# Matrix sums of a hybrid block's MLP moved from GpSimd to VectorE, and its second query/key group moved ahead

## The chip, the cores and the metric

The kernel runs on one core of a Trainium2 chip. The engines are TensorE (PE, matrix products; PEld is its weight load), VectorE (DVE), ScalarE (ACT), GpSimd (POOL) and SyncE (SP, which issues most loads). The metric is device time in microseconds (us), lower is better.

## What is computed

One decoder block on 512 tokens of width 1024, in float32: an RMS norm, one wide input projection, two causal token mixers side by side, a gated sum, an output projection with residual, and a squared-ReLU MLP with residual.

```python
p = rms_norm(x, norm_mix_g) @ w_in
q_a, k_a, v_a, o_a, i_a, f_a, q_b, k_b, v_b, g_a, g_b = split(p)
qk_a = silu(causal_conv([q_a, k_a], conv_w))          # 4 taps
h_a = mlstm_chunkwise(*heads(qk_a), v_a, i_pre, f_pre)  # 8 heads, 64-wide keys
y_a = sigmoid(o_a) * head_rms_norm(h_a)
y_b = stick_breaking(norm(q_b), norm(k_b), v_b)       # 8 heads, 128 wide
y = sigmoid(g_a) * y_a + sigmoid(g_b) * y_b
x = x + y @ w_out
h2 = rms_norm(x, norm_mlp_g)
x = x + square(relu(h2 @ w_up)) @ w_down              # 1024 -> 4096 -> 1024
```

## The kernel before

Every matrix product is done in split precision. Each float32 operand is held as a rounded part (hi) and a remainder (lo), and `mm3` (L110 to L113) issues three matmuls for one product: hi with hi, hi with lo, lo with hi. Weights come in pieces of 512 KB: `stage` (L95) loads a piece into a buffer "raw" of which there are two, ACT copies it rounded (`whi`, L106), and DVE subtracts to get the remainder (`wlo`, L107). The second matmul group on a piece can't start before both are there.

The first part of the program is the projections and the mixers. They are cut into steps that the list `ORDER` names: `qka0`, `qka1` project the queries and keys of mLSTM heads 0 to 3 and 4 to 7 (four banks of PSUM each, evicted by ACT into `xc`, L332, then a convolution on DVE into tiles `cy` with tag "sy"); `r0` to `r7` (`decay`, L369) load a row of gate sums over all partitions into one of three places with tag "f5", mask it on POOL and take the exponential on ACT; `m0` to `m7` are mLSTM heads (`za` scores, multiplied with `rb` on DVE, split into `ph` and `pl`, then `pn`, evicted by ACT into `yq`, L410); `n0` and `n4` norm four heads; `qkb0` to `qkb3` project queries and keys of two stick-breaking heads each (four PSUM banks, evicted by DVE into `nat`, L450, normed with a square root on ACT over `ssq`); `T0` to `T3` transpose them on PE (`pt_qT`, `pt_kT`); `s0` to `s7` are stick-breaking heads; `va1`, `vb0`, `vb1` project values; `oa`, `ga`, `gb` project gates. `ORDER` is the order in which the program is written. A scheduler then orders the instructions of each engine by a simulated timeline, with offsets of priority for evictions and weight pieces, so the order on an engine is near that of `ORDER` but not the same.

The MLP is cut into four quarters g = 0 to 3 of 1024 hidden columns. Each of its products, 512 x 1024 by 1024 x 1024, is done as seven products of half size (Winograd's form, `wino`, L649), on sums and differences of the quadrants: for the weights POOL issues loads that add into a buffer already there (L661), which are then split again (`parts`, L632: `whi_p..` on ACT, L635, `wlo_p..` on DVE, L636). For the operand, `rows_rest` (L553) makes four sums S1 to S4 of quadrants in place, in tiles `uq` (in the first call `hq`), and splits each. It is called twice for the normed input `h2` and twice in each quarter, ten times in all. Up and down products of neighbouring quarters alternate on PE. In the names `wlo_p2up21`, p2 is the product's number, up or dn the matrix, 2 the quarter and 1 the half of the piece; `xdn`, `ydn`, `zdn` and `pp_xup`, `pp_yup`, `pp_zup` are PSUM sums, `s` and `acc` what they are added to (`add`, L692). I call the stretch where quarter g's hidden rows are made and the next products wait for them boundary g.

Of the kernel before, what the change touches and what calls it, by code (L numbers as in the profile page):

```python
# [51 lines left out]
ORDER = ("qka0 r0 r1 qka1 r2 r3 qkb0 m0 r4 m1 m2 r5 m3 r6 n0 va1 T0 m4 m5 qkb1 vb0 r7 m6 oa0 s0 m7 T1 s1 ga0 "  # L52
         "n4 s2 s3 qkb2 T2 qkb3 vb1 T3 s4 s5 oa1 gb0 s6 s7 x0 ga1 gb1").split()
# [3 lines left out]
def block_kernel(ctx: ExitStack, tc: tile.TileContext, x, norm_mix_g, w_in, b_if, b_gate, conv_w, mlstm_norm_g,  # L57
# [35 lines left out]
    last, load_pool = {}, [(wp, "raw", 2)]  # L93

    def stage(k2, srcs, name, ahead=None, pool_raw=None):  # L95

        with tc.high_priority(offset=AHEAD if ahead is None else ahead):
            p, tag, bufs = load_pool[0] if pool_raw is None else (pool_raw, "raw", 2)
            raw = p.tile([P, 2, 512], F32, tag=tag, name=f"raw_{name}{k2}", bufs=bufs)
            for c, ap in srcs:  # L100
                n = ap.shape[-1]
                last["load"] = nc.sync.dma_start(out=raw[:, :, c:c + n],
                                                 in_=ap.rearrange("(kk p) n -> p kk n", p=P)).ins
            hi = wp.tile([P, 2, 512], F32R, tag="whi", name=f"whi_{name}{k2}")
# [221 lines left out]
    def qka(i):  # L326
# [6 lines left out]
        y = [t2("sy", 5, f"cy{i}{o}") for o in range(4)]  # L333
# [49 lines left out]
    def mlstm_head(h, qk, v, rb):  # L383
# [16 lines left out]
        s = t2("sy", 5, f"s{h}")  # L400
# [73 lines left out]
    def sb_head(h, q, k, v):  # L474
# [34 lines left out]
        yb = t2("sy", 5, f"yb{h}")  # L509
# [43 lines left out]
    def rows_rest(A, q, a21, a22, *sl):  # L553
# [4 lines left out]
        pool.tensor_tensor(p["S3"], p["A11"], a21, ALU.subtract)  # L558
        pool.tensor_tensor(p["S2"], p["S1"], p["A11"], ALU.subtract)
        pool.tensor_tensor(p["S4"], p["A12"], p["S2"], ALU.add)  # L560
# [58 lines left out]
    load_pool[0] = (rd, "rawd", 8)  # L619
# [231 lines left out]
```

## Time and profile before

| | before |
|---|---|
| median of 3 runs | 845.93 us (845.5 to 846.26) |
| profiled run, device time | 846.01 us |
| span of its trace | 844.3 us |
| PE busy | 815.5 us (97%) |
| DVE busy | 632.4 us (75%) |
| ACT busy | 442.0 us (52%) |
| POOL busy | 217.7 us (26%) |

The span is the time from the first to the last instruction in the trace of one execution; the device time holds 1.7 us more. Busy shares are means over stages. PE's ends are modelled, so the share says how much of the span it had work in hand, not that it ran at its peak.

### The profile page before, as it was taken

The numbers are of one execution on the slowest core, as the hardware profiler recorded it, in microseconds if no ns is written. First come the engines' busy times: TensorE is split into PE (matmuls) and PEld (weight loads), VectorE is DVE, ScalarE is ACT, GpSimd is POOL, SyncE is SP. The second block draws the span as 40 slices with busy tenths as digits, with TensorE's granted clock in tenths as the row PEclk, the third lists the DMA queues.
The fourth block names the chain that finished last, engine by engine and source line by source line (L and its number), as shares of the span: only waits on it lengthen the run. The fifth ranks groups of instructions, "written<-read, shape, count | busy, mean of one in ns | idle before, by whom it ended". The sixth has DMA issues, their size and how long they took to land.

```text
span 844.3 us, 11460 instructions
## 1 busy us (share of the span) xinstructions
PE 815.5 (97%) x4366; PEld 697.1 (83%) x4366; DVE 632.4 (75%) x785; ACT 442.0 (52%) x649; POOL 217.7 (26%) x244
## 2 busy tenths in 40 slices
PE   7999998999999999999999998999999999999987
PEld 5877777788888788888888888988997999899766
DVE  5577999796548687645764659898689778988994
ACT  6337567755436564443553456666456545555521
POOL 3014145141211110011120106174216421641530
PEclk9999999999999999999999999999999999999999
DMA  8155343474233242431349406878956996698365
GB/s 206 48 129 173 94 122 104 99 176 81 45 81 100 51 125 76 100 74 53 82 133 330 102 23 176 201 150 173 222 165 142 203 221 165 132 212 212 50 115 135
DMA packets 62760, 111.54 MB, mean 132 GB/s; under 512 B 5161, under 2 KB 17497, under 8 KB 62706
## 3 DMA queue, kind: packets, MB, share of 16 engines
q1 hardware_dynamic: 43122, 69.32, 29.3%
q0 software_dynamic: 19584, 41.50, 25.6%
q8 instruction: 34, 0.56, 0.3%
q14 instruction: 20, 0.16, 0.1%
HBM read 108.63 MB, written 2.17 MB: 131 GB/s over the span
## 4 chain that ended last, share of the span: by engine, by line
PE 68%; DVE 14%; DMA 7%; issue 5%; ACT 4%; POOL 1%; SPq 0%; POOLq 0%; ACTq 0%; DVEq 0%
PE pp_qkb L111 3%; PE pp_qkb L112 3%; PE pp_qkb L113 3%; DMA raw_qka<-in_w_in_dram 2%; PE ydn L111 2%; PE pp_yup L111 2%; PE ydn L112 2%; PE ydn L113 2%; PE pp_yup L112 2%; PE pp_yup L113 2%; PE pp_vb L111 2%; PE pp_ga L111 2%; PE pp_ga L113 2%; PE pp_gb L112 2%; PE pp_ga L112 2%
## 5 line engine op out<-in xcount | busy, mean ns | idle before, releaser
L487 POOL TENSOR_SCALAR_AFFINE_SELECT b<-b 128x128 f32<-128x128 f32 x32 | 20.9, 674 | 171.2 <-ACT b L484 171.2
L661 POOL DMA_DIRECT2D raw_Xup<-in_w_up_dram x24 | 29.1, 1230 | 110.6 <-DVE wlo_p1up L636 57.5
L661 POOL DMA_DIRECT2D raw_Xdn<-in_w_down_dram x24 | 29.5, 1241 | 90.6 <-DVE wlo_p5dn L636 30.0
L112 PE MATMUL pp_qkb<-wlo_qkb,hT 128*128 128x512 f32 x128 | 50.0, 391 | 0.0
L111 PE MATMUL pp_qkb<-whi_qkb,hT 128*128 128x512 f32 x128 | 50.0, 392 | 0.0
L113 PE MATMUL pp_qkb<-whi_qkb,hT 128*128 128x512 f32 x128 | 49.4, 391 | 0.0
L492 DVE TENSOR_TENSOR_SCAN r<-r,msk 128x512 f32<-128x512 f32 (+3 forms) x32 | 25.4, 835 | 14.3 <-ACT r L483 14.3
L113 PEld LDWEIGHTS pp_qkb<-whi_qkb,hT 128*128 128x128 f32 x128 | 24.0, 188 | 5.5
L112 PEld LDWEIGHTS pp_qkb<-wlo_qkb,hT 128*128 128x128 f32 x128 | 24.0, 188 | 5.3
L111 PEld LDWEIGHTS pp_qkb<-whi_qkb,hT 128*128 128x128 f32 x128 | 24.0, 188 | 5.2
L784 ACT ACTIVATE uq<-uq 128x512 f32<-128x512 f32 x32 | 20.1, 631 | 14.8 <-DVE uq L783 14.6
L111 PE MATMUL pp_va<-whi_va,hT 128*128 128x512 f32 x64 | 25.5, 404 | 1.4 <-DVE nat L450 1.4
L111 PE MATMUL pp_vb<-whi_vb,hT 128*128 128x512 f32 x64 | 25.0, 392 | 0.7 <-DVE nat L450 0.7
L112 PE MATMUL pp_va<-wlo_va,hT 128*128 128x512 f32 x64 | 25.5, 399 | 0.0
L113 PE MATMUL pp_va<-whi_va,hT 128*128 128x512 f32 x64 | 25.5, 399 | 0.0
L111 PE MATMUL pp_qka<-hT,whi_qka 128*128 128x512 f32 x64 | 24.9, 395 | 0.4 <-ACT xc L332 0.4
L401 POOL COPY s<-rb 128x128 f32<-128x128 f32 x8 | 4.3, 543 | 81.5 <-DVE rb L396 81.5
L112 PE MATMUL pp_qka<-hT,whi_qka 128*128 128x512 f32 x64 | 25.2, 393 | 0.0
L111 PE MATMUL pp_gb<-hT,whi_gb 128*128 128x512 f32 x64 | 25.1, 393 | 0.0
L112 PE MATMUL pp_wo<-wlo_wo,y 128*128 128x512 f32 x64 | 25.1, 392 | 0.0
L112 PE MATMUL pp_gb<-hT,whi_gb 128*128 128x512 f32 x64 | 25.1, 391 | 0.0
L112 PE MATMUL pp_ga<-hT,whi_ga 128*128 128x512 f32 x64 | 25.0, 391 | 0.0
(556 smaller groups left out, 3049.9 us busy)
## 6 DMA issues: line engine op xcount, KB each, us to landing
raw_Xup<-in_w_up_dram POOLq DMA_DIRECT2D x24, 512.0 KB, 8.3
raw_Xdn<-in_w_down_dram POOLq DMA_DIRECT2D x24, 512.0 KB, 6.9
raw_qkb<-in_w_in_dram SPq DMA_DIRECT2D x32, 256.0 KB, 3.7
rb<-rows POOLq DMA_DIRECT2D x8, 640.0 KB, 4.7
raw_va<-in_w_in_dram SPq DMA_DIRECT2D x8, 512.0 KB, 5.3
raw_qka<-in_w_in_dram SPq DMA_DIRECT2D x16, 256.0 KB, 4.8
raw_vb<-in_w_in_dram SPq DMA_DIRECT2D x8, 512.0 KB, 4.6
raw_oa<-in_w_in_dram SPq DMA_DIRECT2D x8, 512.0 KB, 4.3
```

The costliest lines, as they stand in the source:

```text
L111: pe.matmul(o, ah, bh, start=start, stop=False, **kw)
L112: pe.matmul(o, ah, bl, start=False, stop=False, **kw)
L113: pe.matmul(o, al, bh, start=False, stop=stop, **kw)
L401: pool.tensor_copy(s[:, :P], rb[:, :P])
L487: pool.affine_select(out=b[:, d], in_=b[:, d], pattern=[[-1, P]], compare_op=ALU.is_gt, fill=0.0, base=0, channel_multiplier=1)
L492: dve.tensor_tensor_scan(kr, kr, msk[:, S - n:][:, ::-1], 1.0, ALU.mult, ALU.max)
L661: pool.dma_start(out=buf[b, j], in_=src(more, j), accum_op=ALU.add)
L784: act.activation(h(r, c), h(r, c), AF.Square)
```

## The change

Five things are changed.

1. In `rows_rest`, the sums S3, S2 and S4 are made on DVE in place of POOL: three in each of ten calls.
2. `ORDER` is written anew. `qkb0` takes the place behind `qka0` that `qka1` had, `qkb1` follows soon, the first four heads of both mixers (m0 to m3, s0 to s3) come ahead of `qka1`, and heads 4 to 7 follow.
3. From `qkb1` on, every third weight piece goes to an additional buffer, in the pool `at`, so that there are three.
4. The tag "sy" (convolution outputs, row sums, stick-breaking outputs) has eight places, not five.
5. The residual tiles `acc` 2 and 3 lie in another pool and are loaded later; and `r3` no longer waits for `qka1`.

```diff
--- before.py
+++ after.py
@@ -49,8 +49,8 @@
 C_QB, C_KB, C_VB, C_GA, C_GB = 3088, 4112, 5136, 6160, 7184
 
 
-ORDER = ("qka0 r0 r1 qka1 r2 r3 qkb0 m0 r4 m1 m2 r5 m3 r6 n0 va1 T0 m4 m5 qkb1 vb0 r7 m6 oa0 s0 m7 T1 s1 ga0 "
-         "n4 s2 s3 qkb2 T2 qkb3 vb1 T3 s4 s5 oa1 gb0 s6 s7 x0 ga1 gb1").split()
+ORDER = ("qka0 r0 r1 qkb0 m0 r2 m1 r3 T0 qkb1 m2 m3 n0 vb0 s0 T1 s1 oa0 s2 s3 qka1 ga0 r4 r5 va1 m4 r6 m5 r7 qkb2 m6 m7 "
+         "n4 T2 qkb3 vb1 s4 s5 T3 gb0 s6 s7 x0 oa1 ga1 gb1").split()
 
 
 @with_exitstack
@@ -90,12 +90,13 @@
         return at.tile([P, S], F32, tag=tag, name=name, bufs=bufs)
 
 
-    last, load_pool = {}, [(wp, "raw", 2)]
+    last, load_pool, staged = {}, [(wp, "raw", 2)], []
 
     def stage(k2, srcs, name, ahead=None, pool_raw=None):
 
         with tc.high_priority(offset=AHEAD if ahead is None else ahead):
-            p, tag, bufs = load_pool[0] if pool_raw is None else (pool_raw, "raw", 2)
+            p, tag, bufs = load_pool[len(staged) % len(load_pool)] if pool_raw is None else (pool_raw, "raw", 2)
+            staged.append(name)
             raw = p.tile([P, 2, 512], F32, tag=tag, name=f"raw_{name}{k2}", bufs=bufs)
             for c, ap in srcs:
                 n = ap.shape[-1]
@@ -330,7 +331,7 @@
             xc = [t2("nat", 4, f"xc{i}{o}") for o in range(4)]
             for o, a in enumerate(accs):
                 taken = act.copy(xc[o], a).ins
-        y = [t2("sy", 5, f"cy{i}{o}") for o in range(4)]
+        y = [t2("sy", 8, f"cy{i}{o}") for o in range(4)]
         for j in range(4):
             for o in range(4):
                 w = col(24 + (0, 4)[o // 2] + 2 * i + o % 2 + 8 * (3 - j))
@@ -397,7 +398,7 @@
         for e in (slice(0, 512), slice(512, LIN)):
             act.copy(ph[:, e], rb[:, e])
             dve.tensor_sub(pl[:, e], rb[:, e], ph[:, e].bitcast(F32))
-        s = t2("sy", 5, f"s{h}")
+        s = t2("sy", 8, f"s{h}")
         pool.tensor_copy(s[:, :P], rb[:, :P])
         pool.tensor_tensor(s[:, P:], rb[:, P:S], rb[:, OFF[1]:OFF[1] + 384], ALU.add)
         pool.tensor_tensor(s[:, 256:], s[:, 256:], rb[:, OFF[2]:OFF[2] + 256], ALU.add)
@@ -506,7 +507,7 @@
         for j, o, n in sorted(SEG):
             mm3(po[:, j * P:], v[j][:, 0, c], v[j][:, 1, c], ah[:, o:o + n], al[:, o:o + n], j == 0, j == 3,
                 skip_group_check=True)
-        yb = t2("sy", 5, f"yb{h}")
+        yb = t2("sy", 8, f"yb{h}")
         act.copy(yb, po)
         return yb
 
@@ -555,16 +556,15 @@
         p = {n: q(*ROWS[n])[:, *sl] for n in ROWS}
         dve.tensor_sub(p["S1"], a21, a22)
         rows_split(A, "S1", p["S1"], *sl)
-        pool.tensor_tensor(p["S3"], p["A11"], a21, ALU.subtract)
-        pool.tensor_tensor(p["S2"], p["S1"], p["A11"], ALU.subtract)
-        pool.tensor_tensor(p["S4"], p["A12"], p["S2"], ALU.add)
+        dve.tensor_sub(p["S3"], p["A11"], a21)
+        dve.tensor_sub(p["S2"], p["S1"], p["A11"])
+        dve.tensor_add(p["S4"], p["A12"], p["S2"])
         for n in ("S4", "S2", "S3"):
             rows_split(A, n, p[n], *sl)
 
 
-    late = ExitStack()
+    late, heads = ExitStack(), ExitStack()
     at = late.enter_context(tc.tile_pool(name="at", bufs=1, reuse_waits="tile"))
-    heads = ExitStack()
     ah_ = heads.enter_context(tc.tile_pool(name="ah", bufs=1, side="right", reuse_waits="tile"))
     msk = at.tile([P, S], F32, name="msk")
     pool.memset(msk, 0.0)
@@ -576,10 +576,12 @@
 
     def step(n):
         kind, i = n[:-1], int(n[-1])
+        if n == "qkb1":
+            load_pool[:] = [(wp, "raw", 2), (at, "raw", 1), (wp, "raw", 2)]
         if kind == "qka":
             got[n] = qka(i)
         elif kind == "r":
-            got[n] = decay(i, got["qka1"][3] if i > 2 else got["qka0"][4])
+            got[n] = decay(i, got["qka1"][3] if i > 3 else got["qka0"][4])
         elif kind == "m":
             got[n] = mlstm_head(i, got[f"qka{i // 4}"], (v0, v1)[i // 4], got[f"r{i}"])
         elif kind == "n":
@@ -605,9 +607,14 @@
         step(n)
     heads.close()
     rd = ctx.enter_context(tc.tile_pool(name="rd", bufs=1, side="right", reuse_waits="tile"))
-    acc_t = [rd.tile([P, D], F32, name=f"acc{t}") for t in range(NT)]
-    for t in range(NT):
-        nc.gpsimd.dma_start(out=acc_t[t], in_=x[0, t * P:(t + 1) * P, :])
+
+    def residual(p, ts):
+        for t in ts:
+            acc_t.append(p.tile([P, D], F32, name=f"acc{t}"))
+            nc.gpsimd.dma_start(out=acc_t[t], in_=x[0, t * P:(t + 1) * P, :])
+
+    acc_t = []
+    residual(rd, (0, 1))
     for n in ORDER[ORDER.index("x0") + 1:]:
         step(n)
     late.close()
@@ -616,7 +623,8 @@
 
 
     mp = ctx.enter_context(tc.tile_pool(name="mp", bufs=1, reuse_waits="tile"))
-    load_pool[0] = (rd, "rawd", 8)
+    load_pool[:] = [(rd, "rawd", 8)]
+    residual(mp, (2, 3))
     h2a = [big.tile([P, 4, 4, HT], F32R, tag=f"hT{i}", name=f"h2{i}") for i in range(2)]
     H2 = {n: (h2a[i // 2][:, 2 * (i % 2)], h2a[i // 2][:, 2 * (i % 2) + 1]) if i < 4 else
           tuple(mp.tile([P, 4, HT], F32R, name=f"h2{n}{w}") for w in "hl") for i, n in enumerate(ROWS)}
```

What that does to the order of instructions is shown at three places. The first is DVE at the start of the second query/key group. Before, behind the first mLSTM query/key group (names ending in 00 and 01) DVE goes on with the convolution of `qka1` (`cy10` and on):

```order
L358 TENSOR_TENSOR kk00_617<-cy02_590,kk00_617 64x512 x2
L356 TENSOR_TENSOR ql01_633<-cy01_589,qh01_631 64x512 x2
L107 TENSOR_TENSOR wlo_qkb02_982<-raw_qkb02_978,whi_qkb02_981 128x1024
L358 TENSOR_TENSOR kk01_632<-cy03_591,kk01_632 64x512 x2
L338 TENSOR_SCALAR cy10_818<-xc10_810,vec_108 128x512
L338 TENSOR_SCALAR cy11_819<-xc11_811,vec_108 128x512
L338 TENSOR_SCALAR cy12_820<-xc12_812,vec_108 128x512
L396 SCALAR_TENSOR_TENSOR rb0_646<-za0_0_1067,rb0_646 128x512
```

After, DVE has the same four pieces of work first, and then the four evictions of `qkb0` (`nat00` to `nat03`, from the banks `pp_qkb00` to `pp_qkb03`), on which the banks of the next projection depend:

```order
L359 TENSOR_TENSOR kk00_617<-cy02_590,kk00_617 64x512 x2
L357 TENSOR_TENSOR ql01_633<-cy01_589,qh01_631 64x512 x2
L108 TENSOR_TENSOR wlo_qkb12_1053<-raw_qkb12_1049,whi_qkb12_1052 128x1024
L359 TENSOR_TENSOR kk01_632<-cy03_591,kk01_632 64x512 x2
L451 COPY nat00_811<-pp_qkb00_682 128x512
L451 COPY nat01_816<-pp_qkb01_683 128x512
L451 COPY nat02_821<-pp_qkb02_684 128x512
L451 COPY nat03_826<-pp_qkb03_685 128x512
L397 SCALAR_TENSOR_TENSOR rb0_646<-za0_0_837,rb0_646 128x512
L397 SCALAR_TENSOR_TENSOR rb0_646<-za0_1_838,rb0_646 128x512
L108 TENSOR_TENSOR wlo_qkb13_1084<-raw_qkb13_1080,whi_qkb13_1083 128x1024
```

What moved: the projection that follows on PE is now `qkb1`, whose first matmul needs a bank that DVE frees; before, PE went on to `qkb0` in banks that ACT freed.

The second place is ACT ahead of the transposes T0 (their `pt_` tiles), after the change. `rb3` is the decay row of mLSTM head 3, `ssq0` the square sums of `qkb0`, and `yq0` with `pn1` the eviction of mLSTM head 1:

```order
L381 ACT_TABLE_LOAD
L381 ACTIVATE rb3_933<-rb3_933,cc_389 128x512
L107 CAST whi_vb00_1294<-raw_vb00_1292 128x1024
L456 ACT_TABLE_LOAD
L456 ACTIVATE ssq0_810<-ssq0_810,eps_89 128x16
L381 ACT_TABLE_LOAD
L381 ACTIVATE rb3_933<-rb3_933,cc_389 128x384
L381 ACTIVATE rb3_933<-rb3_933,cc_389 128x128
L381 ACTIVATE rb3_933<-rb3_933,cc_389 128x256
L107 CAST whi_vb01_1324<-raw_vb01_1322 128x1024
L411 COPY yq0_440<-pn1_919 128x512
L468 ACTIVATE qT0_956<-pt_qT0_951,vec_108 128x512
```

Before, the decay rows' exponentials stood together at rows 81 to 85 of ACT, and no square root or weight piece stood among them:

```order
L380 ACT_TABLE_LOAD
L380 ACTIVATE rb3_894<-rb3_894,cc_389 128x512
L380 ACTIVATE rb3_894<-rb3_894,cc_389 128x384
L380 ACTIVATE rb3_894<-rb3_894,cc_389 128x128
L380 ACTIVATE rb3_894<-rb3_894,cc_389 128x256
L353 CAST qh10_846<-cy10_818 64x512 x2
L452 ACTIVATE njk00_1043<-nat00_1041 128x512
L106 CAST whi_va13_1445<-raw_va13_1443 128x1024
L410 COPY yq0_440<-pn0_1092 128x512
```

What moved: the eviction of head 1's bank now stands behind `rb3`'s exponentials and two loads of activation tables.

The third place is DVE at boundary 1, in the MLP. Before, between the first sum (L556) and the second half of `wlo_p2up2`:

```order
L556 TENSOR_TENSOR uq11_4896<-uq10_4895,uq11_4896 128x2x256
L693 TENSOR_TENSOR s11_4013<-s11_4013,xdn11_5694 128x512
L636 TENSOR_TENSOR wlo_p2dn10_5794<-raw_Zdn10_5677,whi_p2dn10_5793 128x1024
L636 TENSOR_TENSOR wlo_p2dn11_5798<-raw_Zdn11_5679,whi_p2dn11_5797 128x1024
L551 TENSOR_TENSOR uS11l_4904<-uq11_4896,uS11h_4903 128x512
L551 TENSOR_TENSOR uS41l_4906<-uq11_4896,uS41h_4905 128x512
L551 TENSOR_TENSOR uS21l_4908<-uq10_4895,uS21h_4907 128x512 x2
L551 TENSOR_TENSOR uS31l_4910<-uq10_4895,uS31h_4909 128x512 x2
L636 TENSOR_TENSOR wlo_p2up20_5828<-raw_Zup20_5725,whi_p2up20_5827 128x1024
L693 TENSOR_TENSOR acc0_3704<-acc0_3704,xdn10_5693 128x512
L551 TENSOR_TENSOR uS41l_4906<-uq11_4896,uS41h_4905 128x512
L636 TENSOR_TENSOR wlo_p2up21_5832<-raw_Zup21_5727,whi_p2up21_5831 128x1024
```

After (line numbers of the changed kernel: L559, L560 and L561 are the three moved sums, L552 and L644 the splits):

```order
L644 TENSOR_TENSOR wlo_p2dn10_5794<-raw_Zdn10_5677,whi_p2dn10_5793 128x1024
L561 TENSOR_TENSOR uq11_4896<-uq11_4896,uq10_4895 128x2x256
L644 TENSOR_TENSOR wlo_p2dn11_5798<-raw_Zdn11_5679,whi_p2dn11_5797 128x1024
L559 TENSOR_TENSOR uq10_4895<-uq10_4895 128x2x256
L552 TENSOR_TENSOR uS11l_4904<-uq11_4896,uS11h_4903 128x512
L552 TENSOR_TENSOR uS41l_4906<-uq11_4896,uS41h_4905 128x512
L552 TENSOR_TENSOR uS21l_4908<-uq10_4895,uS21h_4907 128x512
L560 TENSOR_TENSOR uq10_4895<-uq11_4896,uq10_4895 128x2x256
L552 TENSOR_TENSOR uS31l_4910<-uq10_4895,uS31h_4909 128x512 x2
L644 TENSOR_TENSOR wlo_p2up20_5828<-raw_Zup20_5725,whi_p2up20_5827 128x1024
L561 TENSOR_TENSOR uq11_4896<-uq11_4896,uq10_4895 128x2x256
L644 TENSOR_TENSOR wlo_p2up21_5832<-raw_Zup21_5727,whi_p2up21_5831 128x1024
```

What moved: the sums stand among the splits (two more of this call's neighbour stand a few rows ahead), and part of `uS41l`, `uS21l` and the `acc` addition now come behind the second `wlo_p2up2`. On POOL the rows of L558 to L560 are gone; its loads of L661 keep their order.

## Rows read from the trace of the kernel before


**Rows 1.** The head of the page: the span, and each engine's busy time, share of the span and instructions.

```profile
span 844.3 us, 11460 instructions
...
PE 815.5 (97%) x4366; PEld 697.1 (83%) x4366; DVE 632.4 (75%) x785; ACT 442.0 (52%) x649; POOL 217.7 (26%) x244
```

**Rows 2.** Busy time by stretch: from and to in us, its length, then PE, PEld, DVE, ACT, POOL busy us with instructions, granted clock of PE, DMA share, GB/s. The mixers, a quiet stretch of the MLP, and boundary 1.

```profile
160.00:480.00 320.00, 319.21 (x1556) 267.05 (x1555) 209.37 (x266) 158.83 (x250) 45.23 (x61) 1.00 0.40 106
...
580.00:640.00 60.00, 60.00 (x387) 54.82 (x386) 46.13 (x55) 28.96 (x34) 18.93 (x16) 1.00 0.92 195
640.00:660.00 20.00, 17.99 (x116) 15.87 (x115) 19.50 (x20) 12.46 (x20) 10.01 (x7) 1.00 0.59 140
```

**Rows 3.** PE's waits from 60 to 460 us (mixers): line that waited, engine, tile and line waited for, us in total, times, longest.

```profile
PE za L389 <- ACT yq L410: 1.5, 1, 1.5
PE pp_va L111 <- DVE nat L450: 1.4, 1, 1.4
PE za L389 <- DVE kk L358: 1.3, 1, 1.3
PE pn L112 <- DVE pl L399: 1.2, 1, 1.2
PE pp_vb L111 <- DVE nat L450: 0.7, 1, 0.7
```

**Rows 4.** PE's waits from 490 to 845 us (MLP), same columns, the five largest.

```profile
PE pp_xup L113 <- DVE wlo_p2up L636: 3.9, 3, 2.0
PE xdn L111 <- DVE s L693: 3.0, 1, 3.0
PE p L729 <- DVE xh L726: 2.5, 2, 1.5
PE pp_zup L113 <- DVE wlo_p5up L636: 1.2, 1, 1.2
PE zdn L111 <- ACT whi_p5dn L635: 1.2, 1, 1.2
```

**Rows 5.** Instructions of single lines over the whole span: the sum that DVE makes already, and a maximum on DVE; ns shortest/median/longest, first and last start.

```profile
L556 DVE TENSOR_TENSOR uq<-uq,uq x8: 679/684/2039, 554.3 to 789.7; 128x512 f32<-128x512 f32 x8
...
L783 DVE TENSOR_SCALAR uq<-uq x24: 414/426/1518, 539.0 to 786.5; 128x512 f32<-128x512 f32 x24
```

**Rows 6.** DVE's groups of instructions from 632 to 650 us (boundary 1): count, then busy us, mean ns of one, idle before.

```profile
L636 DVE TENSOR_TENSOR wlo_p2dn<-raw_Zdn,whi_p2dn 128x1024 fp32r<-128x1024 f32 x2 | 4.2, 2124 | 0.0
L551 DVE TENSOR_TENSOR uS11l<-uq,uS11h 128x512 fp32r<-128x512 f32 x2 | 4.0, 2015 | 0.0
L551 DVE TENSOR_TENSOR uS41l<-uq,uS41h 128x512 fp32r<-128x512 f32 x1 | 1.8, 1778 | 0.0
L783 DVE TENSOR_SCALAR uq<-uq 128x512 f32<-128x512 f32 x1 | 1.5, 1514 | 0.0
...
L551 DVE TENSOR_TENSOR uS21l<-uq,uS21h 128x512 fp32r<-128x512 f32 x2 | 1.3, 678 | 0.0
```

**Rows 7.** The timeline at boundary 1, DVE and then POOL: start us, duration us, engine, line, operation.

```profile
651.39 1.21 DVE L636 TENSOR_TENSOR wlo_p2up<-raw_Zup,whi_p2up 128x1024 fp32r<-128x1024 f32 x1
...
653.13 0.68 DVE L551 TENSOR_TENSOR uS41l<-uq,uS41h 128x512 fp32r<-128x512 f32 x1
653.73 1.21 DVE L636 TENSOR_TENSOR wlo_p2up<-raw_Zup,whi_p2up 128x1024 fp32r<-128x1024 f32 x1
...
646.89 1.62 POOL L560 TENSOR_TENSOR uq<-uq,uq 128x512 f32<-128x512 f32 x1
```

**Rows 8.** DVE's timeline where h2 is made: the same pair of instructions for the second and the third block of rows (the one with no POOL sums beside it, the other with them).

```profile
504.95 1.40 DVE L726 SCALAR_TENSOR_TENSOR xh<-acc,ss,gain 128x512 f32<-128x512 f32 x2
...
511.13 4.57 DVE L726 SCALAR_TENSOR_TENSOR xh<-acc,ss,gain 128x512 f32<-128x512 f32 x2
```

**Rows 9.** Busy time by stretch, columns as in rows 2, right behind the waits at h2 and at boundary 3.

```profile
515.00:518.60 3.60, 2.75 (x13) 2.78 (x14) 3.60 (x5) 2.04 (x4) 1.75 (x2) 0.53 1.12 235
...
805.30:808.70 3.40, 2.91 (x7) 2.33 (x8) 3.40 (x6) 0.00 (x0) 1.21 (x1) 0.50 0.00 0
```

**Rows 10.** The timeline at the end of the first mLSTM query/key group: PE, DVE and ACT.

```profile
91.80 0.39 PE L111 MATMUL pp_qkb<-whi_qkb,hT 128*128 128x512 f32 x1
...
93.74 1.41 DVE L358 TENSOR_TENSOR kk<-cy,kk 64x512 fp32r<-64x512 f32 x2
...
92.48 1.06 ACT L106 CAST whi_qkb<-raw_qkb 128x1024 fp32r<-128x1024 f32 x1
```

**Rows 11.** The timeline of the decay row rb3, POOL and then ACT.

```profile
105.29 0.58 POOL L372 DMA_DIRECT2D rb<-rows  x1 [3.87 <-issue]
109.33 4.56 POOL L374 TENSOR_SCALAR_AFFINE_SELECT rb<-rb 128x128 f32<-128x128 f32 x4 [3.47 <-DMA rb<-rows]
...
112.56 0.63 ACT L342 ACTIVATE xc<-cy 128x512 f32<-128x512 f32 x1
113.21 1.28 ACT L380 ACT_TABLE_LOAD   x1
114.50 1.93 ACT L380 ACTIVATE rb<-rb,cc 128x512 f32<-128x512 f32 x4
...
119.73 0.57 ACT L410 COPY yq<-pn 128x512 f32<-128x512 f32 x1
```

**Rows 12.** DMA issues: KB each, median us from issue to landing, of the adding loads.

```profile
raw_Xup<-in_w_up_dram POOLq DMA_DIRECT2D x24, 512.0 KB, 8.3
```

## The prediction

> **What bounds the kernel now.** I read the head of the page, then busy time by stretch, then PE's waits with the instructions beside them. PE is busy for 815.5 of 844.3 us, DVE for 632.4 [rows 1]. From 160 to 480 us PE has work for 319.2 of 320 us, and in a quiet stretch of the MLP for 60 of 60 [rows 2]: there the matmuls alone set the time, and the change leaves their number as it is. So time can come only from the places where PE stands. In the mixers these are five waits of 0.7 to 1.5 us [rows 3]. In the MLP they are a chain of larger ones, at h2 and at the four boundaries, nearly all for a result of DVE: 3.9 us for `wlo_p2up`, 3.0 for `s`, 2.5 for `xh`, 1.2 for `wlo_p5up`, and 1.2 for ACT's `whi_p5dn` [rows 4]. At boundary 1, DVE is busy for 19.5 of 20 us while PE is idle for 2 [rows 2]: DVE is the bound there.
>
> The reader should see why DVE is late there. The same form of split, 128 x 512, takes 0.68 us for `uS21l` but 2.02 for `uS11l` and 1.78 for `uS41l`; the piece `wlo_p2dn` takes 2.12 us where `wlo_p2up` takes 1.21; a maximum takes 1.51 where its median is 0.43 [rows 5 to 7]. The slow ones lie beside POOL's sums; the last of those at boundary 1 runs from 646.89 to 648.5, and a `uS41l` of the same form at 653.13 is back at 0.68 [rows 7].
>
> **Part 1, the sums on DVE.** Added: 30 sums. DVE makes one such sum already, L556, in 0.68 us [rows 5]; an instruction of its form starts at 653.13 and the next one at 653.73, 0.60 later [rows 7]. That is 3.6 us for six at a boundary, at most 6 x 0.684 = 4.1, and 18 to 20.5 in all. Taken away at boundary 1: 2 x (2.02 - 0.68) = 2.7 on `uS11l`, 1.1 on `uS41l`, 2 x (2.12 - 1.21) = 1.8 on `wlo_p2dn`, 1.51 - 0.43 = 1.1 on the maximum, together 6.7 us. So DVE should come through it 6.7 - 3.6 = 3.1 us sooner, with more to do.
>
> Now each wait. *Boundary 1*: PE waited 2.0 us, the longest of three, for the first half of `wlo_p2up2`, which ended at 651.39 + 1.21 = 652.6 [rows 4, 7]. After the change five of the six sums stand ahead of it, and one of two `uS21l` behind it: 652.6 - 6.7 + 5 x 0.6 - 0.6 = 648.3. PE wants it at 652.6 - 2.0 = 650.6. The wait goes, with 2.3 us to spare: 2.0 saved. *Boundary 0*: the other two waits for `wlo_p2up`, 3.9 - 2.0 = 1.9, of the same making: 1.9. *Boundary 2*: 1.2 for `wlo_p5up`, less than the 3.1: 1.2. *h2*: the pair `xh` took 4.57 us beside POOL's sums and 1.40 without them [rows 8]: 3.2 sooner, less one sum of 0.6 ahead of it, against waits of 2.5 together [rows 4]: 2.5. *Boundary 3*: `s` 3.0 us late, DVE 3.1 sooner: 3.0, and some 0.5 of a small wait for `acc` just ahead; the 1.2 for `whi_p5dn` hangs on a load and stays: 3.5. Sum 11.1.
>
> **The clock.** Behind the waits at h2 and at boundary 3 the granted clock was 0.53 and 0.50, so the lower level of 1.2 GHz, for 3.6 and 3.4 us, with PE busy for 2.75 and 2.91 of these [rows 9]. PE had mostly stood before each. At the full clock this work takes half the time: at most 1.4 and 1.5 lost; since the first matmuls overlap the wait I take 1.1 each. If both waits go the falls should go too: 2.2, bounds 0 to 2.9.
>
> What is late next is the adding loads, which POOL issues when DVE's split has freed their buffer and which take 8.3 us to land [rows 12]. PE reaches each product sooner, so I give back 1.0, about the one wait of this kind that shows now (1.2) [rows 4]. MLP: -11.1 - 2.2 + 1.0 = -12.3.
>
> **Part 2, the second query/key group.** Before, `qkb0` started at 91.80 in banks which ACT had freed, while DVE was at `kk` until 93.74 + 1.41 = 95.15 [rows 10]. Now `qkb1` starts here, and its first bank is freed by DVE's `nat00`, behind that same `kk`: 95.15 + 0.7 (a 128 x 512 copy at the time of L556 [rows 5]) + 0.2 for the start is 96.0, so PE waits 96.0 - 91.8 = 4.2 us, where nothing waited. Bounds: 0, if DVE has run ahead because `qka1`'s convolution is no longer in between; 6, with a clock fall like those above behind it. I add 0.6 for a fall at odds of one half.
>
> Next, T0. Head 1's bank, which the last transposes reuse, is freed by ACT behind `rb3`'s exponentials. In the trace that row's load was issued at 105.29, its mask ended at 109.33 + 4.56 = 113.9, and the exponentials took 1.93 behind a table load of 1.28 [rows 11]. Now the load needs the place of `rb0`, whose last reader stands behind the late `nat` copies; I put its issue near 103, so the mask ends near 111.6. Behind that ACT has a first exponential (0.6), two weight casts of 1.06 [rows 10], two table loads of 1.28, the rest of the exponentials (1.3) and the eviction (0.57) [rows 11], 7.2 us, thus 118.8. PE gets there near 117.0 (96.0 and 21 us of matmuls, heads and transposes). Wait 1.8, bounds 0 and 4.5 (nothing late, or the load at 105.3 as now).
>
> One page speaks against this. In the trace an exponential starts at 114.50, right where the table load ends (113.21 + 1.28), and the load starts right where the activation before it ends, 112.56 + 0.63 [rows 11]. The Trainium skill, "ScalarE: Activation LUTs", section "What ACT_TABLE_LOAD costs", puts a drain of about 1380 ns on top of 1283 ns for each change of set. By it, as an estimate, two loads would make the wait at T0 some 2.8 us longer and the sum 839; the trace shows the 1283 ns and no drain.
>
> Removed in the mixers: the waits of 1.5 (`za` for `yq`), 1.4 (`pp_va` for `nat`) and 1.2 (`pn` for `pl`), whose neighbours now stand elsewhere, 4.1 us. The 1.3 for `kk` is kept, since its producers are the same, and so is the 0.7 for `nat` before `pp_vb`, since `vb1` still follows `qkb3` [rows 3]. Mixers: -4.1 + 4.2 + 0.6 + 1.8 = +2.5.
>
> **Parts 3 to 5 at nothing.** The third buffer, the "sy" places and the later `acc` loads change when transfers start; PE misses 0.8 us in 320 [rows 2], so there is nothing to gain there, and if their cover fails a late piece costs what a wait in rows 3 costs, about 1.5. Five more table loads are 6.4 us on ACT, which is busy for 158.8 of those 320 [rows 2].
>
> **Sum.** 846.0 (this execution; it is the median within 0.1) - 12.3 + 2.5 = 836.2 us.
>
> **The rivals.**
> *The loads take over.* Half of the 13.3 saved in the MLP comes back as waits for the adding loads: +5.6 on top of the 1.0, 842. For it: 8.3 us to landing, and PE already waits once for such a piece [rows 4, 12]. Against it: DVE's splits, which release the loads, come sooner too. The Trainium skill, "SBUF — State Buffer", section "SBUF: two separate sides", says that POOL can't write a load's descriptors while DVE runs certain operations; more DVE operations would make this rival likelier, and no row here shows by how much.
> *The new waits are covered.* DVE and ACT run early enough for `qkb1` and T0: 836.2 - 4.2 - 0.6 - 1.8 = 829.6.
> *The drain.* If the change of table set costs what no row shows, 1.4 more at each of two loads ahead of T0: 839, inside the forecast's own range.
> *Nothing hidden is freed.* The boundaries' waits hang on loads alone, the sums were hidden on POOL, and DVE's slow rows were no loss: then only the mixers count, 846.0 + 2.5 = 848.5. Against it: PE's waits name DVE, and 19.5 of 20 us busy [rows 2].
> *The other side: DVE's slow rows are not POOL's doing.* Then six sums cost 3.6 us at each of five boundaries where DVE is the bound, 18 us, and the waits grow: up to 846.0 + 2.5 + 18 = 866. It decides where a boundary gives back under 3.6 us of slow rows; boundary 1 shows 6.7. Against it: `xh` has both times in one form, 6 us apart [rows 8].
>
> **How the numbers follow.** Forecast 0.60, its own range 831 to 839.5 (the wait at `qkb1` from 0 to 6, T0 from 0 to 4.5, the clock from 0 to 2.9, not all at one end); the drain 0.03; the loads 0.18; covered 0.07; nothing freed 0.07; the other side 0.05. I predict 836. The range is 829.5 to 843: it takes in the forecast, the covered case and the loads, and leaves out the two slow cases and tails, under 2 in 10. A measurement of this kernel can tell 0.2%, 1.7 us, from no change: faster is below 844.2. That holds in the forecast, the drain, the covered case and most of the loads: 0.86. Within it: 0.04, the tail of the loads and of nothing freed. Slower: 0.10.
>
> **What would show it.** In the trace after: splits of 128 x 512 at 0.68 in all boundaries and `xh` pairs at 1.4 each; no PE wait for `wlo_p2up`, and `s` under 1 us; the clock at 1.00 behind h2 and boundary 3; a new wait of `pp_qkb` for `nat` of about 4 us near 92 us, and one of `pt_kT` for `yq` near 120. The prediction is wrong if DVE stays slow at the boundaries without POOL's sums, if the waits there name `whi` pieces or loads, or if the mixers lose more than 6 us, as a wait repeated in each head would make them.

## The result and the profile after

The changed kernel takes 836.24 us (835.68 to 837.24, 4 runs), the kernel before 845.71 us (845.07 to 846.26, 4 runs): a ratio of 0.989, interval 0.9872 to 0.9907, faster by 9.5 us. The forecast was 836, with a sum of 836.2. The sum is that near because several of its terms missed in opposite directions, as the trace shows.

The changed kernel's profiled execution took 837.24 us with a span of 835.5 us; this is the head of its page, and its busy time by stretch, with the columns of [rows 2]:

```profile
span 835.5 us, 11477 instructions
...
PE 815.7 (98%) x4366; PEld 697.9 (84%) x4366; DVE 611.4 (73%) x815; ACT 449.6 (54%) x654; POOL 157.5 (19%) x214
```

```profile
160.00:480.00 320.00, 317.19 (x1531) 264.42 (x1530) 213.41 (x275) 166.64 (x261) 47.47 (x80) 1.00 0.40 112
...
640.00:660.00 20.00, 19.79 (x124) 17.76 (x123) 17.82 (x24) 14.50 (x21) 4.83 (x4) 1.00 0.79 179
```

PE's busy time is as before, 815.7 against 815.5 us [rows 1]. DVE has thirty instructions more and is busy for 21.0 us less. Around boundary 1 PE works for 19.8 of 20 us, where it was 18.0 [rows 2]; from 160 to 480 us, in the mixers, it stands for 2.8 us where it stood for 0.8.

The two halves part cleanly at the first matmul of the output projection. The rows below give, for one line's matmuls on a tile, the count, the ns (shortest/median/longest) and the first and last start; before, and then after:

```profile
L111 PE MATMUL pp_wo<-whi_wo,y x64: 389/389/397, 460.6 to 505.3; 128*128 128x512 f32 x64
...
L111 PE MATMUL pp_qka<-hT,whi_qka x64: 388/389/504, 42.9 to 88.3; 128*128 128x512 f32 x64
```

```profile
L112 PE MATMUL pp_wo<-whi_wo,y x64: 389/389/398, 463.0 to 507.7; 128*128 128x512 f32 x64
...
L112 PE MATMUL pp_qka<-hT,whi_qka x64: 388/389/504, 42.5 to 215.5; 128*128 128x512 f32 x64
```

From the first `qka0` to the first `pp_wo`, the mixers, it was 460.6 - 42.9 = 417.7 us and is 463.0 - 42.5 = 420.5: +2.8 (forecast +2.5). From there to the end it was 844.3 - 460.6 = 383.7 and is 835.5 - 463.0 = 372.5: -11.2 (forecast -12.3). Up to `qka0` it is -0.4, a difference that other runs of the same code show too. I use these two lengths for every run below and call them *mixers* and *rest*. Split into PE's standing and PE's work, the mixers' 2.8 us are 0.3 of standing and 2.5 of work (411.1 us before, 413.5 after), and the 11.2 of the rest are 8.6 of standing and 2.6 of work (366.2 and 363.6). The matmuls are the same, so the differences in work are times in which PE took longer over them; the clock, below, is one reason.

PE's waits after, from 60 to 480 us, with the columns of [rows 3]:

```profile
PE pp_qkb L112 <- DVE nat L451: 3.8, 1, 3.8
PE pn L112 <- ACT ph L399: 1.1, 1, 1.1
PE pp_gb L112 <- DVE vb L170: 0.7, 1, 0.7
PE zb L112 <- DVE qT L469: 0.6, 1, 0.6
PE pp_va L112 <- ACT g_ga L528: 0.5, 2, 0.3
PE za L390 <- DVE kk L359: 0.3, 1, 0.3
```

and from 480 us on, which answers to [rows 4]:

```profile
PE pp_yup L112 <- ACT uq L777: 1.6, 1, 1.6
PE ydn L112 <- DVE acc L701: 1.2, 1, 1.2
PE zdn L113 <- DVE wlo_p5dn L644: 0.8, 1, 0.8
PE pp_yup L112 <- DVE uq L783: 0.7, 1, 0.7
PE pp_xup L114 <- DVE wlo_p2up L644: 0.5, 1, 0.5
PE zdn L112 <- ACT whi_p5dn L643: 0.2, 1, 0.2
```

In the MLP the waits for `s`, `xh` and `wlo_p5up` are gone and that for `wlo_p2up` is down from 3.9 to 0.5 us. In the mixers the forecast wait of `pp_qkb` for `nat` is there, and the one at T0 is not.

Why DVE is earlier shows in its groups of instructions from 632 to 655 us, beside [rows 6]:

```profile
L644 DVE TENSOR_TENSOR wlo_p2dn<-raw_Zdn,whi_p2dn 128x1024 fp32r<-128x1024 f32 x2 | 2.4, 1223 | 0.0
...
L561 DVE TENSOR_TENSOR uq<-uq,uq 128x512 f32<-128x512 f32 x2 | 1.4, 692 | 0.0
...
L552 DVE TENSOR_TENSOR uS41l<-uq,uS41h 128x512 fp32r<-128x512 f32 x2 | 1.4, 690 | 0.0
L552 DVE TENSOR_TENSOR uS11l<-uq,uS11h 128x512 fp32r<-128x512 f32 x2 | 1.4, 690 | 0.0
```

`wlo_p2dn` takes 1.22 us, not 2.12, the splits 0.69, not 1.78 to 2.02, and a moved sum 0.69, where POOL took 1.62 [rows 7].

### The profile page after: what moved, and what is told of

Its sections match the earlier page's. It is cut to its first block, busy times and chain, and to the rows that moved or that the text cites. A ratio compares the mean times of both kernels' runs of the same rounds, so it can differ in the third digit from the quotient of the medians.

```text
span 835.5 us, 11477 instructions
## 1 busy us (share of the span) xinstructions
PE 815.7 (98%) x4366; PEld 697.9 (84%) x4366; DVE 611.4 (73%) x815; ACT 449.6 (54%) x654; POOL 157.5 (19%) x214
## 4 chain that ended last, share of the span: by engine, by line
PE 78%; DVE 8%; DMA 5%; ACT 5%; issue 3%; SPq 0%; POOL 0%; ACTq 0%; DVEq 0%
PE pp_yup L112 3%; PE pp_yup L113 3%; PE pp_yup L114 3%; PE pp_qkb L112 3%; PE pp_qkb L114 3%; PE pp_qkb L113 3%; PE ydn L114 2%; PE ydn L113 2%; PE ydn L112 2%; DMA raw_qkb<-in_w_in_dram 2%; PE pp_gb L112 2%; PE pp_zup L112 2%; PE pp_zup L113 2%; PE pp_ga L113 2%; PE pp_ga L112 2%
## 5 line engine op out<-in xcount | busy, mean ns | idle before, releaser
L112 PE MATMUL pp_qkb<-whi_qkb,hT 128*128 128x512 f32 x128 | 50.8, 402 | 3.8 <-DVE nat L451 3.8
L488 POOL TENSOR_SCALAR_AFFINE_SELECT b<-b 128x128 f32<-128x128 f32 x32 | 18.4, 597 | 172.1 <-ACT b L485 156.4
L114 PE MATMUL pp_qkb<-whi_qkb,hT 128*128 128x512 f32 x128 | 50.6, 399 | 0.0
L108 DVE TENSOR_TENSOR wlo_qkb<-raw_qkb,whi_qkb 128x1024 fp32r<-128x1024 f32 x16 | 19.4, 1223 | 16.3 <-ACT whi_qkb L107 16.3
L107 ACT CAST whi_qkb<-raw_qkb 128x1024 fp32r<-128x1024 f32 x16 | 16.6, 1049 | 17.7 <-DMA raw_qkb<-in_w_in_dram 14.2
L112 PE MATMUL pp_gb<-hT,whi_gb 128*128 128x512 f32 x64 | 24.9, 391 | 0.7 <-DVE vb L170 0.7
L114 PE MATMUL pp_oa<-hT,wlo_oa 128*128 128x512 f32 x64 | 25.2, 393 | 0.0
L113 PE MATMUL pp_oa<-hT,whi_oa 128*128 128x512 f32 x64 | 25.1, 392 | 0.0
```

What stands on the lines that cost most here:

```text
L112: pe.matmul(o, ah, bh, start=start, stop=False, **kw)
L113: pe.matmul(o, ah, bl, start=False, stop=False, **kw)
L114: pe.matmul(o, al, bh, start=False, stop=stop, **kw)
L488: pool.affine_select(out=b[:, d], in_=b[:, d], pattern=[[-1, P]], compare_op=ALU.is_gt, fill=0.0, base=0, channel_multiplier=1)
```

## The experiments

Each run was compared with the kernel before on the same chip (e1 to e4, e5 to e8, and e9, e10 and e7b together); its medians there were 845.3, 846.7 and 846.2 us, so ratios compare better than microseconds. Mixers and rest come from the one profiled execution of each; these two columns are no averages.

| kernel | us | ratio to before (interval) | mixers | rest |
|---|---|---|---|---|
| before | 845.71 | 1 | 417.7 | 383.7 |
| the change | 836.24 | 0.989 (0.9872 to 0.9907) | 420.5 | 372.5 |
| e1, sums back on POOL | 848.85 | 1.0038 (1.0024 to 1.0052) | 421.1 | 385.3 |
| e2, sums on DVE alone | 832.67 | 0.9849 (0.9832 to 0.9865) | 417.7 | 371.3 |
| e3, no sums at all | 830.04 | 0.9818 (0.9801 to 0.9834) | 417.2 | 368.6 |
| e4, `nat` of `qkb0` on ACT | 833.60 | 0.9854 (0.9837 to 0.9872) | 416.9 | 372.1 |
| e5, `za0` three times | 835.72 | 0.9872 (0.9857 to 0.9886) | 419.5 | 372.6 |
| e6, change with old order | 833.63 | 0.9846 (0.9829 to 0.9862) | 417.7 | 372.9 |
| e7, two load buffers | 840.14 | 0.9919 (0.9903 to 0.9936) | 422.8 | 371.0 |
| e7b, the same again | 837.89 | 0.9898 (0.9878 to 0.9918) | 421.3 | 373.1 |
| e8, e2 with `nat` on ACT | 837.68 | 0.9898 (0.9881 to 0.9915) | 422.3 | 372.2 |
| e9, e2 with relu first | 829.58 | 0.9806 (0.9792 to 0.9821) | 416.8 | 368.6 |
| e10, e4 with relu first | 830.44 | 0.9815 (0.9801 to 0.983) | 419.0 | 368.9 |

The granted clock is part of what these two columns show. In the mixers it fell to 0.50 for some us behind the wait of 3.8 us for `nat` in the change, e1, e7 and e7b, behind one of 1.8 us for `vb` in e7 and e10, and behind one of 2.1 us for `dh` in e8. In the rest it fell at boundary 3 in the kernel before, the change, e1, e4, e7b and e8, at h2 in the kernel before and at boundary 1 in e1. The traces of e2, e3, e5, e6 and e9 show no fall in either, up to the last matmul.

**The sums, undone and alone.** In the changed kernel the three lines go back:

```diff
-        dve.tensor_sub(p["S3"], p["A11"], a21)
-        dve.tensor_sub(p["S2"], p["S1"], p["A11"])
-        dve.tensor_add(p["S4"], p["A12"], p["S2"])
+        pool.tensor_tensor(p["S3"], p["A11"], a21, ALU.subtract)
+        pool.tensor_tensor(p["S2"], p["S1"], p["A11"], ALU.subtract)
+        pool.tensor_tensor(p["S4"], p["A12"], p["S2"], ALU.add)
```

> The changed kernel with the thirty sums back on POOL; the rest of the change stays. Theory (POOL's sums slow DVE's instructions beside them, and that made PE wait at h2 and the boundaries): the trace of the changed kernel has 11.3 us less lost time behind 480 us than the kernel before, and that comes back: 847.5 us (846 to 849.5), with splits of 128x512 at 1.78 beside the sums and waits for wlo_p2up, xh and s of 10 us or more together. Rival (the gain came from the new order or the new place of the residual tiles): the time stays near 836 whatever engine makes the sums.

Measured: 848.85 us, slower than before. The rest is back at 385.3 us and the mixers stay at 421.1. These are PE's waits behind 480 us in that kernel, and DVE's groups at boundary 1:

```profile
PE pp_xup L114 <- DVE wlo_p2up L644: 4.8, 3, 2.2
PE xdn L112 <- DVE s L701: 3.0, 1, 3.0
PE p L737 <- DVE xh L734: 2.5, 2, 1.5
PE pp_zup L114 <- DVE wlo_p5up L644: 1.2, 1, 1.2
```

```profile
L644 DVE TENSOR_TENSOR wlo_p2dn<-raw_Zdn,whi_p2dn 128x1024 fp32r<-128x1024 f32 x2 | 4.2, 2122 | 0.0
L552 DVE TENSOR_TENSOR uS11l<-uq,uS11h 128x512 fp32r<-128x512 f32 x2 | 4.0, 2012 | 0.0
```

The slow rows of [rows 6] come back, and so do the waits of [rows 4] (3.0, 2.5 and 1.2 to the digit, and 4.8 for `wlo_p2up` where it was 3.9), with the new order in place. So the new order brings no gain without the sums.

The other way round, the same three lines in the kernel before, with nothing else changed:

> The kernel before with the thirty sums on DVE and nothing else changed. Theory: the MLP gains what it gained in the whole change, 11.3 us, and the mixers stay as they were: 834.4 us (832.5 to 836), below the whole change, whose mixers lost some 2.5 to 3.5 us. Rival (the new order is needed for the gain, or gives a part of it): 838 or above.

Measured: 832.67 us. The mixers are 417.7 us, as before, and the rest 371.3. The sums alone give 12.4 us of rest, and they give more than the whole change does. The other parts, taken together, cost some 3.5 us by the ratios.

**What the sums cost on DVE.** The kernel before without the three lines, on no engine, so that it leaves out a part of the MLP:

> The kernel before without the thirty sums S3, S2 and S4 on any engine: their splits and products run on the unsummed quadrants. It takes away POOL's slowing of DVE and also DVE's 18 us for the sums. Theory (in the changed kernel those 18 us lie beside PE's work, and DVE is the bound no longer): only 0 to 1.5 us below the kernel with the sums alone on DVE, 833 to 834.4 us. Rival (DVE is still the bound at the five boundaries, and each sum on it costs its 0.6): 816 to 828 us.

Measured: 830.04 us, 2.6 below e2, with a rest 2.7 us shorter. That is more than I expected, and outside the 816 to 828 of the rival. The 2.7 is a difference of two orders and no bound for the cost of the sums: without them the scheduler puts other splits ahead of `xh`, and e3's trace has a wait of 2.8 us for `xh` and 1.6 us for the piece `p6dn`, which e2's has not, while e2's 1.6 at `pp_yup` is gone. Even with these 4.4 us added, 30 sums of 0.60 us, 18 us of DVE, cost PE some 7 us by this estimate: more than half of them lie beside PE's work. The 70 splits of 128 x 512 in the MLP take 0.67 to 2.93 us in the kernel before, and 0.67 to 0.70 in e2, in the change and in e3, which has no sums on either engine.

**The wait at the second group.** In the changed kernel, `qkb0`'s evictions on the other engine:

```diff
-                dve.tensor_copy(n, acc[t])
+                (act.copy if p == 0 else dve.tensor_copy)(n, acc[t])
```

> The changed kernel with the four evictions of qkb0 on ACT in place of DVE. In the changed kernel PE waits 3.8 us for the first of them, and the granted clock is 0.50 for about 5 us behind that wait, some 2.4 us lost. Theory (the wait is DVE's queue of splits ahead of the eviction, and the fall of the clock belongs to the wait): ACT is free there, both go, 830 us (829 to 832.5). Rival (ACT's own queue, or the transposes T0 behind it, take the wait over): 834 to 838.

Measured: 833.60 us, between the two. The trace shows both things gone: on PE the last `za` and the first `pp_qkb` of the second group stand side by side, where the changed kernel had 3.8 us between them.

```profile
89.72 0.28 PE L392 MATMUL za<-ql,kk 128*128 128x256 f32 x1
89.84 0.40 PE L112 MATMUL pp_qkb<-whi_qkb,hT 128*128 128x512 f32 x1
```

The mixers are 3.6 us shorter, not 6.2 (3.8 of the wait and 2.4 of the clock, below). Part of it is given back: `za` for `kk` 0.8 us instead of 0.3, `pn` for `pl` 0.6, and later `pp_gb` for `vb` 1.3 instead of 0.7, together 1.7. So the wait was DVE's queue, as the theory says. The waits that grow are for results of DVE and not, as the rival has it, for ACT's queue or T0, and they do not account for the whole difference.

**The clock behind that wait.** First the changed kernel's row for the stretch behind the wait, columns as in [rows 9], and the spacing of its matmuls on PE's timeline:

```profile
93.40:98.70 5.30, 5.25 (x12) 4.12 (x13) 5.27 (x9) 1.89 (x3) 2.25 (x3) 0.50 0.37 76
```

```profile
96.17 0.63 PE L112 MATMUL pp_qkb<-whi_qkb,hT 128*128 128x512 f32 x1
96.60 0.63 PE L113 MATMUL pp_qkb<-wlo_qkb,hT 128*128 128x512 f32 x1
...
99.24 0.39 PE L114 MATMUL pp_qkb<-whi_qkb,hT 128*128 128x512 f32 x1
99.47 0.40 PE L112 MATMUL pp_qkb<-whi_qkb,hT 128*128 128x512 f32 x1
```

At a granted clock of 0.50, the lower level of 1.2 GHz, a matmul comes every 0.43 us, at the full one every 0.23. Twelve of them lose 12 x 0.20 = 2.4 us, which is nearly all of the 2.5 us by which PE's work in the mixers grew. To see whether the standing engine brings this on, PE is given work in the wait:

```diff
-        for j, o, n in SEG:
+        for j, o, n in SEG * (3 if h == 0 else 1):
```

> The changed kernel, with the eight score matmuls of head 0 (za0) done three times over instead of once, with the same result: sixteen more matmuls, 2.9 us by the trace of the changed kernel, all ahead of PE's 3.8 us wait for the eviction of qkb0. The wait's end is set by DVE and stays where it is. Theory (the granted clock falls to 0.50 for 5 us because PE stands in that wait, and costs 2.4 us): PE stands for only 1 us, the clock stays at 1.00, and the time falls, with more work done, to 833.8 us (833 to 835.2). Rival (the fall has another cause): 836.2. Rival (the repeats hold up head 0's results or the eviction): 837 to 839.

```profile
92.97 0.50 PE L112 MATMUL pp_qkb<-whi_qkb,hT 128*128 128x512 f32 x1 [1.29 <-DVE nat L451]
93.31 0.40 PE L113 MATMUL pp_qkb<-wlo_qkb,hT 128*128 128x512 f32 x1
93.54 0.39 PE L114 MATMUL pp_qkb<-whi_qkb,hT 128*128 128x512 f32 x1
```

The trace does what the theory says: PE stands for 1.3 us, and behind it matmuls come every 0.23 us at once. All four traces with the wait of 3.8 us (the change, e1, e7, e7b) show the fall, for some 3 to 5 us of PE's work, and the three without it (e4, e5, e10) show none there. The fall is thus shown to belong to the wait. With sixteen matmuls more, the kernel takes 835.72 us, or 0.18% less than the change by the ratios (intervals that overlap), and its profiled mixers are 1.0 us shorter. That the 2.4 us come back as time is not shown; the waits for `vb` (1.5 us instead of 0.7) and for `kk` (0.7 instead of 0.3) take 1.2 of them.

**The buffers and the order apart.** The change with the old list `ORDER` (and the old condition for `r3`), so parts 1, 3, 4 and 5:

> The changed kernel with the list ORDER of the kernel before (and with it r3's old wait); sums on DVE, third load buffer, eight sy places and later acc loads as in the change. Theory (parts 3 to 5 are worth nothing, the order alone cost the mixers 3 to 4 us): as the kernel with the sums alone, 832.7 us (831.5 to 834). Rival (the buffers cost the time, by transfers that start earlier and collide): 835.5 to 837. Rival (they gain by themselves): under 831.5.

Measured: 833.63 us, a ratio of 0.9846 where e2 has 0.9849, and the same 417.7 us of mixers. With the old order the buffers are worth nothing, so the new order is what costs the mixers 2.8 us.

In the new order, the change without its third load buffer:

> The changed kernel without the third load buffer; all else as changed. Theory (no load is waited for in the mixers, with two buffers or three): 836.2 us (835 to 837.5). Rival (the new order needs the third buffer): 838 or more, with PE waits for whi or wlo pieces between 100 and 460 us.

> The kernel with two load buffers in the new order once more, for another profile: its profiled execution took 837.3 us and showed no wait for a load, while the others took 839.4 to 840.6. Theory (with two buffers a weight piece comes late in most executions, and three buffers cover that): a profile at 839 or more, with 2 us of PE waits for whi or wlo pieces in the mixers, or for what follows from them, that the trace of the changed kernel doesn't have. Rival (the difference lies elsewhere, in the MLP's loads or at the start): the mixers as in the profile of the changed kernel.

Measured: 840.14 us, and for the same kernel in another comparison 837.89 us (ratios 0.9919 and 0.9898, against 0.989 for the change). Neither profile is of one of the longer executions: they took 837.3 and 837.6 us, with the waits of `pp_gb` for `vb` at 1.8 and 1.6 us and no wait for a load in the mixers. Behind the 1.8 of e7 the granted clock is 0.50 from 356.8 to 360.2 us, which is part of its 422.8 us of mixers; behind the 1.6 of e7b it stays at 1.00. This stays open: in the new order the third buffer is worth between nothing and 2.5 us by the ratios, and where, I can't say.

**Versions that go further.** The old order with the sums on DVE, and `qkb0`'s evictions on ACT, as in e4:

> The kernel with the sums alone on DVE, and qkb0's four evictions on ACT besides. Its PE waits 1.4 us for the first of these evictions at pp_va, and 1.2 and 1.5 us for pl and yq near it. Theory (DVE's queue holds the eviction up here too): the 1.4 goes and the others stay, 831.3 us (830 to 832.3), the fastest so far. Rival (ACT, which holds the head's eviction yq as well, gets later and the wait for yq grows): 833 to 835.

Measured: 837.68 us. My theory falls, and the rival's direction is right. ACT's timeline there:

```profile
113.09 1.93 ACT L380 ACTIVATE rb<-rb,cc 128x512 f32<-128x512 f32 x4
114.92 1.24 ACT L353 CAST qh<-cy 64x512 fp32r<-64x512 f32 x2
116.19 1.57 ACT L450 COPY nat<-pp_qkb 128x512 f32<-128x512 f32 x3
```

In this order the eviction falls behind an exponential and two casts of `qka1`. Two of PE's waits in the mixers name ACT:

```profile
PE pd L419 <- ACT dh L168: 2.3, 2, 2.1
PE pp_va L111 <- ACT nat L450: 1.5, 1, 1.5
```

The wait of 1.4 us only changes its engine. The one of 2.3 comes up some 37 us later, at 154.4, and behind it the granted clock is 0.50 until 157.7 us. The mixers' 4.6 us over e2 are 2.0 of PE's standing and 2.6 of its work. By the ratios, the same edit gains 3 us in one order and loses 4 in the other. That the eviction gains nothing here is what stands ahead of it in ACT's queue; how the edit brings on the later wait no run shows.

Last, the wait of 1.6 us at `pp_yup` that came up in the MLP. In e2 the last matmul into the bank `pp_xup` starts at 518.78, and ACT begins its eviction at 525.76, behind its copies of the sixth weight piece, which wait; now the piece's splits are kept behind the eviction:

```diff
-                act.activation(h(0, 0), p, AF.Relu)
+                last["relu"] = act.activation(h(0, 0), p, AF.Relu).ins
...
+                    if name == "up0" and n == 6:
+                        es.enter_context(tc.issue_after(last["relu"]))
```

> The kernel with the sums alone on DVE, and in the first up product ACT's eviction of the bank pp_xup (relu) kept ahead of the splits of the sixth weight piece, which wait for an adding load that takes 12 us to land. In its trace PE waits 1.6 us at pp_yup for that eviction, though the bank was complete 5 us sooner. Theory (the wait that came up in the MLP behind the change is the late load, passed on through ACT's queue to a bank that doesn't need the load): the 1.6 goes, and less than 0.5 for the piece itself comes, 831.3 us (830 to 832.3). Rival (PE needs the late piece at the same time anyway, and then waits for whi_p6up): 832.7, with a wait for whi_p6up of 1 to 1.6 us.

Measured: 829.58 us, the fastest here that computes the whole block: 3.1 us below e2, or 3.6 by the ratios, twice what I expected. PE's waits behind 480 us there, all of them:

```profile
PE ydn L111 <- DVE acc L696: 1.2, 1, 1.2
PE zdn L112 <- DVE wlo_p5dn L636: 0.8, 1, 0.8
PE pp_zup L111 <- DVE uq L774: 0.7, 1, 0.7
```

The 1.6 is gone, and none for the piece has come. But the edit also made the scheduler put the product of the third piece ahead of that of the sixth on PE, so that the sixth piece has 5.7 us more (48 matmuls of 0.12). What of the 2.7 us of rest belongs to the eviction and what to this order isn't told apart.

What I expected has one thing wrong: the piece does not wait for its load. In e2 its two adding loads are issued at 508.99 and 510.40 and land 9.8 and 12.2 us later, at 518.8 and 522.6. ACT begins each copy only right behind PE's last matmul on the same half of `whi_p5up`, which holds two of the four `whi` buffers:

```profile
522.98 0.28 PE L112 MATMUL pp_zup<-h,whi_p5up 128*128 128x256 f32 x1
...
523.34 1.05 ACT L635 CAST whi_p6up<-raw_Xup 128x1024 fp32r<-128x1024 f32 x1 [2.72 <-issue]
...
525.76 1.07 ACT L769 ACTIVATE uq<-pp_xup 128x512 f32<-128x512 f32 x2
```

The matmul ends at 523.26, the copy starts at 523.34. For the second half the times are 524.70 and 524.82, and in the change 526.25 and 526.33. So the eviction stood behind a copy that waited for a buffer which PE itself still read.

> The changed kernel with both mends: qkb0's evictions on ACT, and the eviction of pp_xup ahead of the sixth piece's splits. Theory (the two are far apart and add up): 833.6 - 1.4 = 832.2 us (830.8 to 833.5), level with the kernel with the sums alone, or a little below. Rival (the second is worth nothing): 833.6.

Measured: 830.44 us, 3.2 below e4 (3.3 by the ratios), so the two mends add up, and the second is again worth more than expected. Its profiled mixers are 2.1 us longer than e4's, with the clock at 0.50 from 352.8 to 356.1 us, behind a wait for `vb` of 1.8 us where e4's was 1.3.

## Why the prediction was right, and where its terms were not

*The bound.* Right: e1 and e2 show that PE's waits in the MLP came from DVE and DVE's slowness from POOL's sums. DVE did not stand waiting for sums that POOL made late: at boundary 3 of the kernel before DVE was busy for all of the 27 us from 786 to 813, at boundary 1 for 19.5 of 20 [rows 2].

*Boundaries and h2, -11.1.* The four waits of [rows 4] that were to go fell from 10.6 to 0.5 us. The 1.2 for `whi_p5dn` that I kept is 0.2, with 0.8 for the `wlo` of the same piece. The term is right in mechanism and size.

*What the loads give back, +1.0.* Wrong in cause and mis-sized. Four waits have come up: 1.6, 1.2, 0.8 and 0.7, together 4.3 us. The largest is not for an adding load: it is for a bank whose eviction stands in ACT's queue behind a copy that waits for a `whi` buffer which PE still reads (e9). Of the four, only the 0.8 for `wlo_p5dn` has a load behind it in the trace: ACT copies the first half of that piece after 1.4 us of waiting for its load. Smaller waits that I had left out of [rows 4] and that went (three of 0.5 to 0.7) make up for some of it.

*The clock, -2.2.* Half right. Behind h2 the clock is now 1.00; but in e1, where the waits for `xh` are back at 2.5 us, it is 1.00 there too, so these waits alone don't decide it. PE's work in the rest fell by 2.6 us, and how much of that is the clock no run tells apart. At boundary 3 the clock still falls, later:

```profile
810.00:812.00 2.00, 2.00 (x7) 1.52 (x6) 1.15 (x2) 0.00 (x0) 1.61 (x2) 0.50 1.08 258
```

It does so behind the 1.2 us wait for `acc`. In e2, e5 and e9 the same wait stands and the clock stays at 1.00 there; why it falls in one and not in the other, no run shows.

*The second group, +4.2 and 0.6.* The wait is 3.8 us, and its place and its cause are those forecast. The step that failed is the 0.6: I took the loss of [rows 9], 1.1 us, at odds of one half, but the clock fell in all four traces that have this wait, and in the change it stayed low for 5.3 us of PE's work and cost 2.4.

*T0, +1.8.* Wrong: no wait. POOL's mask and ACT's queue there, after:

```profile
101.20 0.57 POOL L373 DMA_DIRECT2D rb<-rows  x1 [0.30 <-POOL s L405]
...
107.18 2.21 POOL L375 TENSOR_SCALAR_AFFINE_SELECT rb<-rb 128x128 f32<-128x128 f32 x4
```

```profile
108.23 1.28 ACT L381 ACT_TABLE_LOAD   x1
109.52 0.72 ACT L381 ACTIVATE rb<-rb,cc 128x512 f32<-128x512 f32 x1
...
111.20 1.28 ACT L456 ACT_TABLE_LOAD   x1
112.50 0.31 ACT L456 ACTIVATE ssq<-ssq,eps 128x16 f32<-128x16 f32 x1
...
116.27 0.58 ACT L411 COPY yq<-pn 128x512 f32<-128x512 f32 x1
```

The load went at 101.2, not 103, and the mask took 2.2 us, not 4.6 [rows 11], so that the eviction ended at 116.9, not 118.8; and PE, held up by the clock, came no earlier. The table loads again show 1.28 us and the next activation right behind. The Trainium skill, "ScalarE: Activation LUTs", section "What ACT_TABLE_LOAD costs", adds a drain of some 1380 ns to each change of set; these rows show none.

*Removed in the mixers, -4.1.* The three waits are gone; so is the 0.7 for `nat` at `pp_vb`, and 1.0 of the 1.3 for `kk`, which I had kept. Against that stand four small new ones (1.1, 0.7, 0.6, 0.5), 2.9 us together, that I had not seen at all. Put together, 3.8 + 2.4 + 2.9 new, and 4.1 + 0.7 + 1.0 + 0.4 gone (the last a wait of `pp_qka` for `xc` at 66.8 us, which [rows 3] leaves out), is +2.9, near the 2.8 measured. So the near hit of +2.5 is luck in part: T0's 1.8 was not there, the clock cost 1.8 more than the 0.6, and the other errors nearly cancel.

*The buffers at nothing.* Right in the old order (e6), open in the new (e7).

*The rivals.* The other side (DVE slow by itself) and the hidden sums fall with e1 and e2. The loads that take over didn't: of the waits that came up in the MLP, 4.3 us, one of 0.8 has a load behind it, and against them 1.7 us of small waits went.

## What to carry to other kernels

A second engine doesn't unload the first when its work slows the first down: POOL's sums cost DVE more (6.7 us at a boundary) than DVE needs to do them (3.6). Compare one form of instruction with and without the other engine beside it before moving work over. And where one part of a change gains 12 and another loses 3, only undoing each alone tells: here the better kernel is the old order with one of five edits.

## What the runs showed of the hardware that I had not expected

A fall of the granted clock can outlast what brought it on: PE stood for 3.8 us, and then ran for 5.3 us at 0.50. Sixteen superfluous matmuls in the wait kept it at 1.00 (e5). And a copy that waits for a buffer can stop PE at a product that doesn't use it, by standing in ACT's queue ahead of an eviction: in e2 the bank had been complete for 6.7 us, and the loads of the piece that was copied had landed, the first 4.5 us before its copy.
